# GpSimd's share of the weight splits, and the order in which the last DeltaNet head puts out its results

## The chip, the core and the metric

The kernel runs as one program on one core of a Trainium2 chip. The metric is the device time of one execution in microseconds; the median of several runs counts. A profile of one execution shows what each engine does: TensorE (PE, with its weight loads as PEld), VectorE (DVE), ScalarE (ACT), GpSimd (POOL) and SyncE (SP), which issues the transfers.

## The reference

Two blocks work one after the other on 256 tokens `x` and 256 tokens of context, each 1024 wide. The first block has two layers of latent attention, a Fourier mix, a Hyena convolution and a squared-ReLU feed-forward net (FFN). The second block has two layers as well. Its first one is a DeltaNet with an FFN, for `x` and for its context; its second one is a gated linear attention (GLA) with an FFN, of which only `x` is put out. The change lies around the DeltaNet, of which this is the core, for chunks of tokens in order:

```python
sol = triangular_solve(eye + m, rhs)          # m: beta * k k^T * decay, strictly lower
v_new = u - einsum('bhid,bhdv->bhiv', w, s)
o = (einsum('bhid,bhdv->bhiv', qc * exp(gcum)[..., None], s)
     + einsum('bhij,bhjv->bhiv', a_qk, v_new))
s = s * exp(gcum[..., -1:])[..., None] + einsum('bhjd,bhjv->bhdv', kc * tail[..., None], v_new)
```

It runs forwards and backwards, first over the context, whose last state `s` starts the run over `x`. Then `o` of both directions is added, normalised over its 128 values, multiplied by `silu(z)` and by the output weights, and added to the stream. After that each stream is normalised over its 1024 values and goes into the FFN, `square(relu(h @ w1)) @ w2`.

## The kernel before

Activations lie with their 1024 features over 128 partitions and 8 slices; the two streams stand side by side in 512 columns, `x` in 0 to 255 and the context in 256 to 511 (`st`, each with its index of the modulation). The dense products are made as three products of rounded parts: `weight` (line 297) loads a block of 128 x 1024 floats into one of three raw buffers, ScalarE rounds it into `wh` (line 307), and line 308 forms the rest, `wl = raw - wh`. That second step is here called a split. It is made by GpSimd if the caller says `pool` or the stage says `pool_lo`, else by VectorE. `mm3` multiplies `wh` with both parts of the input and `wl` with the first, so a block of eight slices and 512 columns takes 24 matmuls.

The order of the instructions on each engine is made by a scheduler when the kernel is built. It takes what is ready by its own estimate of time, in the order of the program where several are ready; each engine then runs its list strictly in that order, and waits where an operand isn't there. `issue_after` sets single instructions behind another one of their engine.

GpSimd makes 91 of the splits: 63 in the DeltaNet (`pool_lo=True` in `run`) and 28 outside, namely the first four blocks of each of the four FFNs (16), the first blocks of the stage that follows an FFN (2 for the first block's second layer, 2 for the DeltaNet, 2 for the GLA), and six of the GLA's projections. It also makes some products of the DeltaNet's `prepare` (lines 1254 and 1256), some of the GLA, and parts of the norm (line 516).

The DeltaNet has eight pairs of heads, called heads here. `project` makes keys, queries and two value tiles of a head (four blocks, each convolved over five taps by VectorE, line 1171), `gates` its two gate tiles (two blocks), `prepare` the decays and the inverse of the small triangular parts (a chain on VectorE, then two trips through memory, `dout` into `TT`, line 1291), `merge` doubles the inverse in three levels, and `steps` runs the four chunks in both directions. `scale` squares the results on ScalarE, takes the inverse root by a chain of small VectorE instructions (`rsqrt`, lines 432 to 438) and multiplies (line 1416). `readout` transposes them, multiplies by the gate and splits them into two parts (tag `r`, four buffers). `write_out` multiplies with two blocks of the output weights and adds to the stream by VectorE (`finish`, line 659). The loop runs over `hd`: merge and steps of head `hd`, `prepare` of the next, `write_out` of the one before, `project` of the one after the next, `readout`, and `gates` of the next.

At `hd == 6` only the first gate tile of the last head is made. The second one and the `write_out` of head six are cut into 24 parts of three matmuls of 512 columns (`late`), which stand between the instructions of head seven's merge (6 parts) and steps (10 parts, line 1388); what is left (8 parts) follows behind `scale`. Then `readout` of head seven needs the four `r` buffers that the parts have read. `write_out(7, og, S, then)` goes over `x` first and the context second: for each, eight results of six matmuls of 256 columns, `finish` with squares and sums for the norm, and then the norm itself (`then`, by `norm_one`). The FFN's first four blocks are multiplied by `lins`, `x` first.

Of the kernel before, what the change touches and what calls it, by code (L numbers as in the profile page):

```python
# [18 lines left out]
P = 128  # L19
# [185 lines left out]
class Net:  # L205
# [91 lines left out]
    def weight(self, src, into=None, pool=False, ahead=False):  # L297
        shp = list(src.shape)
        raw = self.wp.tile(shp, F32, tag="wr", bufs=self.nr_, name="wr")
        self.nc.sync.dma_start(raw, src)  # L300
        wp, nw = (self.wp2, 4) if self.wp2 and not ahead else (self.wp, self.nw)
        if into:
            hi, lo = into
        else:
            hi = wp.tile(shp, F32R, tag="wh", bufs=nw, name="wh")
            lo = wp.tile(shp, F32R, tag="wl", bufs=nw, name="wl")
        self.nc.scalar.copy(hi, raw)  # L307
        (self.nc.gpsimd if pool or self.pool_lo else self.nc.vector).tensor_tensor(lo, raw, hi.bitcast(F32), ALU.subtract)  # L308
        return hi, lo
# [10 lines left out]
    def lin(self, src, rhs, n0, n1, w=None, pool=False):  # L320
        w = w or self.weight(src, pool=pool)
# [231 lines left out]
    def ffn(self, xs, g, w1, w2, mod, tag, streams, ys=None, h=None, quota=0, every=1, S=None, scales=None, before=None, then=None):  # L553
        one = len(streams) == 1
        with ExitStack() as st:
# [5 lines left out]
            ws = [self.weight(self.a[w1][m], pool=True) for m in range(4)]  # L561
# [8 lines left out]
            self.mlp(xs, h, ws, w1, w2, mod, 5, streams, S, scales or {"xc"[v]: 1.0 for (_, _, v) in streams}, before, then, nS)  # L570
# [4 lines left out]
    def mlp(self, xs, h, ws, w1, w2, mod, gch, streams, S, scales, before, then, nS):  # L575
        nc = self.nc
        n = 256 * len(streams)
        for s in range(4):
# [3 lines left out]
            for m in range(0, 8, 2):  # L582
# [13 lines left out]
                elif s == 0 and m == 0:  # L596
                    first = self.lins(ws[:4], h, streams)
# [73 lines left out]
    def pools(self, st, sb, ps, nr, pm, quota=0, pool_lo=False, nwm=2, wide=4, low=()):  # L671
        self.n += 1
        self.pool_lo = pool_lo
# [394 lines left out]
    def deltanet(self, xs, mod, h, ws, first):  # L1068
# [249 lines left out]
        def merge(hd, c, parts):  # L1318
# [30 lines left out]
        def steps(hd, c, parts):  # L1349
# [4 lines left out]
            for step in range(4):  # L1354
                Sn = ap.tile([P, 512], F32, tag="S", bufs=2, name="S") if step < 3 else None
                for d in range(2):
# [31 lines left out]
                    self.between(parts, i.ins, 2 if step == 3 else 1)  # L1388
# [13 lines left out]
                S = Sn  # L1402
            return ot

        def scale(c, ot):
            ss = sp.tile([P, 4, 2], F32, tag="ss", name="ss")
            jk = junk()
            for ch in range(4):
                for v in range(2):
                    nc.scalar.activation(jk, ot[ch // 2][:, 256 * (ch % 2) + P * v : 256 * (ch % 2) + P * v + P], AF.Square,  # L1410
                                         accum_out=ss[:, ch, v : v + 1])
            nc.vector.scalar_tensor_tensor(ss, ss, 1.0 / 128, c["aq"].unsqueeze(2).to_broadcast([P, 4, 2]), ALU.mult, ALU.add)
            so = self.rsqrt(ss.rearrange("p c v -> p (c v)"), [P, 8], "o")
            for p in range(2):
                o = ot[p].rearrange("p (c i) -> p c i", i=P)
                nc.vector.tensor_tensor(o, o, so[:, 4 * p : 4 * p + 4].unsqueeze(2).to_broadcast([P, 4, P]), ALU.mult)
# [11 lines left out]
        def write_out(hd, og, S=None, then=None):  # L1428
            ws = [self.weight(a["dwout"][hd, mq]) for mq in range(2)]
            for sv in st if S else [(0, 512, 0)]:  # L1430
                for m in range(8):
                    c = slice(P * (m % 4), P * (m % 4) + P)
                    wh, wl = ws[m // 4]
                    ps = self.mm_ps()[:, : sv[1] - sv[0]]
                    self.mm3(ps, (wh[:, :, c], wl[:, :, c]), og, sv[0], sv[1])
                    if S:
                        self.finish(xs, m, ps, mod, 2, sv, S, dict(x=1.0, c=1.0))
                    else:
                        for s2 in st:
                            self.finish(xs, m, ps[:, s2[0] : s2[1]], mod, 2, s2, None, None)  # L1440
                if then:
                    then(sv)
# [5 lines left out]
        og, parts = None, iter(())  # L1448
        for hd in range(8):
            if hd == 7:  # L1450
                parts = late(zs, og)
            merge(hd, c, parts)
            ot = steps(hd, c, parts)
            if hd < 7:
                nxt = prepare(hd + 1, *proj)
            if 0 < hd < 7:
                write_out(hd - 1, og)
            if hd < 7:
                tokens(nxt)
# [11 lines left out]
            if hd < 6:  # L1471
                zs = gates(hd + 1)
            elif hd == 6:
                zs = zn
            if hd < 7:
                c = nxt
# [4 lines left out]
        write_out(7, og, S, f["then"])  # L1481
# [4 lines left out]
    def gla(self, xs, mod, h, ws):  # L1486
# [46 lines left out]
        w3 = self.weight(win[2], [vtile().rearrange("p b n -> p (b n)").rearrange("p (k m) -> p k m", k=8).bitcast(F32R) for _ in range(2)], pool=True)  # L1533
# [388 lines left out]
```

## Time and profile before

| | us |
|---|---|
| median of three runs | 2655.13 |
| lowest and highest of them | 2652.54 and 2656.1 |
| the profiled execution's own time | 2648.67 |
| its span, first to last instruction | 2646.9 |

The profile is of one execution of its own, with 1.8 us outside the span. TensorE is busy 2503.5 us of the span, VectorE 1648.9, ScalarE 1133.1 and GpSimd 370.3. The mean granted clock of TensorE is 0.977. The DeltaNet lies from about 1085 to 1853 us, the FFN behind it begins at 1852, and the GLA begins at about 2235. A busy time is an average over stages; what bounds the kernel is read in each stage from the waits of TensorE.

### The profile page before, as it was taken

The page shows a single profiled execution, that of the slowest core. Times are in us where ns is not written, and L with a number is a line of the kernel's source. Part 1 is how long each engine was busy: PE and PEld are TensorE (multiplying, and loading weights), DVE is VectorE, ACT ScalarE, POOL GpSimd, SP SyncE. Part 2 cuts the span into 40 slices and gives each one's busy share as a digit, 9 for nine tenths or more (in the row PEclk, how much of TensorE's full clock was granted, in tenths as well). Part 3 has the DMA queues.
Part 4 walks back from the last instruction along what each step waited for, and adds up shares of the span by engine and source line. Part 5 has one row for each costly group of instructions (what it writes and reads, how often), then busy time and mean ns, then how long its engine had stood idle before and what let it go on. Part 6 is the DMA issues. An engine that isn't in the chain of part 4 may idle for free. (4 is left out here: it accounts for less than half of the span.)

```text
span 2646.9 us, 40579 instructions
## 1 busy us (share of the span) xinstructions
PE 2503.5 (95%) x15740; PEld 2108.8 (80%) x15740; DVE 1648.9 (62%) x3449; ACT 1133.1 (43%) x2161; POOL 370.3 (14%) x268
## 2 busy tenths in 40 slices
PE   7999999999999999988999999977999999899999
PEld 4866877778886999867778877866877888698899
DVE  5555443333567777887877887767533435677676
ACT  3344333232355545663545444534422324564453
POOL 0000200000100100332333323312000001420100
PEclk8999999999999999999999999988999999999999
DMA  7334566663241466222122211211554522222554
GB/s 266 120 117 147 176 254 236 242 236 117 77 141 52 160 194 197 80 66 53 34 61 65 71 39 52 65 35 56 204 179 160 182 88 71 79 93 73 172 184 154
DMA packets 147105, 334.09 MB, mean 126 GB/s; under 512 B 57134, under 2 KB 68512, under 8 KB 146912
## 3 DMA queue, kind: packets, MB, share of 16 engines
q1 hardware_dynamic: 146656, 331.43, 38.6%
q8 instruction: 124, 2.03, 0.3%
q14 instruction: 69, 0.57, 0.1%
q0 software_dynamic: 256, 0.07, 0.0%
HBM read 327.78 MB, written 3.67 MB: 125 GB/s over the span
## 5 line engine op out<-in xcount | busy, mean ns | idle before, releaser
L307 ACT CAST wh<-wr 128x1024 fp32r<-128x1024 f32 (+1 forms) x421 | 426.1, 1016 | 700.2 <-PE pmm L317 511.4
L318 PE MATMUL pmm<-h,wl 128*128 128x512 f32 (+2 forms) x1800 | 624.6, 347 | 16.3 <-DVE wl L308 8.8
L316 PE MATMUL pmm<-h,wh 128*128 128x512 f32 (+2 forms) x1800 | 628.8, 349 | 6.9 <-ACT E L829 1.9
L317 PE MATMUL pmm<-h,wh 128*128 128x512 f32 (+2 forms) x1800 | 621.3, 345 | 0.0
L308 DVE TENSOR_TENSOR wl<-wr,wh 128x1024 fp32r<-128x1024 f32 (+1 forms) x333 | 392.3, 1180 | 288.8 <-ACT wh L307 282.3
L318 PE MATMUL pmm<-r,wl 128*128 128x256 f32 (+1 forms) x1312 | 444.3, 339 | 5.6 <-DVE wl L308 5.5
L316 PE MATMUL pmm<-r,wh 128*128 128x256 f32 (+1 forms) x1312 | 444.9, 340 | 4.5 <-DVE q L989 1.6
L317 PE MATMUL pmm<-r,wh 128*128 128x256 f32 (+1 forms) x1312 | 444.2, 339 | 0.1
L308 POOL TENSOR_TENSOR wl<-wr,wh 128x1024 fp32r<-128x1024 f32 x88 | 216.5, 2465 | 1383.1 <-ACT wh L307 724.4
L318 PEld LDWEIGHTS pmm<-h,wl 128*128 128x128 f32 x1800 | 346.6, 193 | 59.7 <-DVE wl L308 10.2
L316 PEld LDWEIGHTS pmm<-h,wh 128*128 128x128 f32 x1800 | 346.3, 192 | 53.0 <-issue 7.2
L317 PEld LDWEIGHTS pmm<-h,wh 128*128 128x128 f32 x1800 | 346.7, 193 | 37.1 <-issue 0.8
L316 PEld LDWEIGHTS pmm<-r,wh 128*128 128x128 f32 x1312 | 248.4, 190 | 38.7 <-issue 8.9
L318 PEld LDWEIGHTS pmm<-r,wl 128*128 128x128 f32 x1312 | 248.8, 190 | 32.0 <-DVE wl L308 7.0
L317 PEld LDWEIGHTS pmm<-r,wh 128*128 128x128 f32 x1312 | 249.1, 190 | 23.2 <-issue 1.7
L659 DVE SCALAR_TENSOR_TENSOR xs<-pmm,modb,xs 128x256 f32<-128x256 f32 x232 | 106.6, 477 | 133.0 <-PE pmm L318 133.0
L659 DVE SCALAR_TENSOR_TENSOR xs<-pmm,moda,xs 128x256 f32<-128x256 f32 x120 | 54.4, 480 | 146.7 <-PE pmm L318 146.5
L294 ACT CAST r<-h 128x256 fp32r<-128x256 f32 (+1 forms) x128 | 65.5, 513 | 126.8 <-DVE h L610 67.2
L295 DVE TENSOR_TENSOR r<-h,r 128x256 fp32r<-128x256 f32 (+1 forms) x128 | 72.9, 570 | 44.1 <-ACT r L294 40.7
L394 PE MATMUL pmd<-wm,cvs 128*32 128x256 f32 x1408 | 87.2, 382 | 0.0
L1371 ACT COPY e<-pa 128x256 f32<-128x256 f32 x64 | 23.8, 371 | 128.5 <-PE pa L1369 128.0
L394 PEld LDWEIGHTS pmd<-wm,cvs 128*32 128x32 f32 x1408 | 41.1, 109 | 40.1 <-issue 13.4
(484 smaller groups left out, 3834.7 us busy)
## 6 DMA issues: line engine op xcount, KB each, us to landing
wr<-w SPq DMA_DIRECT2D x128, 512.0 KB
wr<-f SPq DMA_DIRECT2D x128, 512.0 KB
wm<-amod SPq DMA_DIRECT2D x24, 2048.0 KB
wr<-dwin SPq DMA_DIRECT2D x49, 512.0 KB
wm<-wmod SPq DMA_DIRECT2D x12, 2048.0 KB
wr<-win SPq DMA_DIRECT2D x28, 512.0 KB
wm<-wmod SPq DMA_DIRECT2D x8, 1536.0 KB
wr<-gwin SPq DMA_DIRECT2D x17, 512.0 KB
```

The lines of the kernel that those rows point to most:

```text
L294: self.nc.scalar.copy(hi, src)
L295: self.nc.vector.tensor_tensor(lo, src, hi.bitcast(F32), ALU.subtract)
L307: self.nc.scalar.copy(hi, raw)
L308: (self.nc.gpsimd if pool or self.pool_lo else self.nc.vector).tensor_tensor(lo, raw, hi.bitcast(F32), ALU.subtract)
L316: mm(ps, wh[:, k, :], rh[:, n0:n1], start=k == 0, stop=False)
L317: mm(ps, wh[:, k, :], rl[:, n0:n1], start=False, stop=False)
L318: self.mark = mm(ps, wl[:, k, :], rh[:, n0:n1], start=False, stop=k == last)
L394: self.last = nc.tensor.matmul(ps[32 * c : 32 * c + 32, :256], cs[:, k + i, :], raw[:, i, 256 * c : 256 * c + 256], start=k + i == 0, stop ...
L659: self.nc.vector.scalar_tensor_tensor(x, ps, mod[:, 8 * gch + m, v : v + 1], x, ALU.mult, ALU.add)
L1371: nc.scalar.copy(vA, ptr[:, :256])
```

## The change

GpSimd's splits outside the DeltaNet go to VectorE (all `pool=True` are taken out). In the DeltaNet `pool_lo` is set by the loop, `0 < hd < 6`: the splits of the turns one to five stay with GpSimd, five turns with eight blocks each, 40 in all. Those ahead of the loop, of turn zero, of turn six and of all that follows go to VectorE. So 51 splits move.

The last head leaves the loop. Both its gate tiles are made in turn six, and `late` keeps only the `write_out` of head six: 16 parts, six of them in the merge and four in steps zero and one. As soon as step one has ended, when both directions have passed the context's chunks, `scale` runs for the context alone, and the one for `x` behind step three. New functions read out one stream (`readout1`, into four free buffers with the tag `D` in place of `r`) and write out one stream (`write_last`). The order is then: context read out, the parts that are left, the context's output product, `x` read out, the context's norm, the output product of `x`, its norm. The FFN's `lins` takes the context first.

The core of the diff; the lines left out take away further `pool` arguments, here and in `run`, and pass `order` on:

```diff
-    def weight(self, src, into=None, pool=False, ahead=False):
+    def weight(self, src, into=None, ahead=False):
...
-        (self.nc.gpsimd if pool or self.pool_lo else self.nc.vector).tensor_tensor(lo, raw, hi.bitcast(F32), ALU.subtract)
+        (self.nc.gpsimd if self.pool_lo else self.nc.vector).tensor_tensor(lo, raw, hi.bitcast(F32), ALU.subtract)
...
-                f["ws"] = [self.weight(w, pool=True, ahead=True) for w in win]
+                f["ws"] = [self.weight(w, ahead=True) for w in win]
...
-            ws = [self.weight(self.a[w1][m], pool=True) for m in range(4)]
+            ws = [self.weight(self.a[w1][m]) for m in range(4)]
...
-                    first = self.lins(ws[:4], h, streams)
+                    first = self.lins(ws[:4], h, order)
...
-        def late(zs, og):
-            def use(ps):
-                zs.append(ap.tile([P, 512], F32, tag="vf", bufs=2, name="z"))
-                nc.scalar.activation(zs[1], ps, AF.Silu)
-
-            yield from self.lin_parts(lambda: self.weight(win[48]), h, 512, use)
+        def late(og):
...
-                    self.between(parts, i.ins, 2 if step == 3 else 1)
+                    if step < 2:
+                        self.between(parts, i.ins)
...
                 S = Sn
+                if step == 1 and half:
+                    half(ot)
             return ot
...
+        def scale(c, ot, streams=(0, 1)):
+            n = len(streams)
...
+            c0 = 2 * streams[0]
+            for ch in range(2 * n):
...
+        def readout1(ot, zs, og, p):
+            pt = self.b_ps()
+            sl = slice(256 * p, 256 * p + 256)
+            for v in range(2):
+                for j in range(2):
+                    self.transpose(pt[:, C(2 * v + j)], ot[p][:, 256 * j + P * v : 256 * j + P * v + P])
+            for v in range(2):
+                z = zs[v][:, sl]
+                nc.vector.scalar_tensor_tensor(z, pt[:, 256 * v : 256 * v + 256], dng[:, 0:1], z, ALU.mult, ALU.mult)
+                self.split(og[v][0][:, sl], og[v][1][:, sl], z)
...
+        def write_last(ws, og, sv, S):
+            for m in range(8):
+                c = slice(P * (m % 4), P * (m % 4) + P)
+                ps = self.mm_ps()[:, :256]
+                self.mm3(ps, [w[:, :, c] for w in ws[m // 4]], og, sv[0], sv[1])
+                self.finish(xs, m, ps, mod, 2, sv, S, dict(x=1.0, c=1.0))
...
-        for hd in range(8):
...
+        for hd in range(7):
+            self.pool_lo = 0 < hd < 6
+            merge(hd, c)
+            ot = steps(hd, c)
...
-            elif hd == 6:
-                zn = [gate(7, 0)]
             else:
-                for part in parts:
-                    part()
+                zn = gates(7)
...
+        parts = late(og)
+        merge(7, c, parts)
+        ot = steps(7, c, parts, lambda ot: scale(c, ot, (1,)))
+        scale(c, ot, (0,))
+        D = lambda: ap.tile([P, 4, P], F32, tag="D", bufs=8, name="og").rearrange("p s i -> p (s i)").bitcast(F32R)
+        og = [(D(), D()) for _ in range(2)]
...
-        write_out(7, og, S, f["then"])
+        readout1(ot, zs, og, 1)
+        for part in parts:
+            part()
+        ws = [self.weight(a["dwout"][7, mq]) for mq in range(2)]
+        write_last(ws, og, st[1], S)
+        with self.tc.issue_after(self.mark.ins):
+            readout1(ot, zs, og, 0)
+        f["then"](st[1])
+        write_last(ws, og, st[0], S)
+        f["then"](st[0])
```

## Rows read from the trace of the kernel before

**Rows 1.** The page: busy us, share of the span, instructions.

```profile
PE 2503.5 (95%) x15740; PEld 2108.8 (80%) x15740; DVE 1648.9 (62%) x3449; ACT 1133.1 (43%) x2161; POOL 370.3 (14%) x268
```

**Rows 2.** Busy time of the engines in four stretches.

```profile
core 0: us, PE busy (x) PEld busy (x) DVE busy (x) ACT busy (x) POOL busy (x), PEclk, DMA share, GB/s
1085.00:1258.00 173.00, 150.11 (x799) 122.68 (x797) 138.43 (x281) 91.27 (x191) 61.11 (x35) 0.93 0.22 61
...
1747.00:1790.00 43.00, 29.38 (x178) 24.84 (x178) 20.52 (x39) 9.96 (x17) 2.34 (x1) 0.80 0.14 25
1813.00:1853.00 40.00, 24.66 (x147) 22.18 (x145) 33.34 (x80) 18.30 (x46) 14.76 (x7) 0.78 0.25 79
...
1880.00:1900.00 20.00, 20.00 (x89) 16.52 (x88) 14.17 (x18) 10.99 (x16) 0.00 (x0) 1.00 0.77 266
```

**Rows 3.** Waits of TensorE, 1813 to 1853 us.

```profile
PE pb L452 <- DVE ot L1416: 11.2, 1, 11.2
PE pb L458 <- DVE rsy L438: 1.6, 1, 1.6
PE pmm L316 <- ACT r L294: 1.1, 1, 1.1
PE pmm L350 <- ACT h L515: 1.0, 1, 1.0
```

**Rows 4.** Timeline, 1818 to 1830 us, VectorE and GpSimd.

```profile
1819.95 0.15 DVE L437 TENSOR_TENSOR rst<-rst,rsh 128x8 f32<-128x8 f32 x1
...
1820.18 9.25 POOL L308 TENSOR_TENSOR wl<-wr,wh 128x1024 fp32r<-128x1024 f32 x4 [2.30 <-ACT wh L307]
...
1824.88 2.27 DVE L437 TENSOR_TENSOR rst<-rst,rsh 128x8 f32<-128x8 f32 x1
```

**Rows 5.** The chain that ended last, 1812 to 1853 us: start, us, what.

```profile
1813.10 0.26 ACT junk L1410
...
1815.66 0.41 ACT junk L1410 x2
...
1833.27 1.01 PE pmm L316 x3
...
1838.63 0.21 PE pmm L318
...
1842.15 0.12 PE pmm L316
...
1852.97 0.58 PE pmm L351
```

**Rows 6.** Waits of TensorE, 1740 to 1790 us.

```profile
PE pb L452 <- DVE ot L1416: 5.9, 1, 5.9
PE pa L1333 <- DMA TT<-dout: 3.6, 1, 3.6
```

**Rows 7.** Line 308: count, then ns as min/median/max.

```profile
L308 DVE TENSOR_TENSOR wl<-wr,wh x333: 409/1225/3355, 50.7 to 2635.3; 128x1024 fp32r<-128x1024 f32 x155, 128x384 fp32r<-128x384 f32 x8, 128x256 fp32r<-128x256 f32 x4
...
L308 POOL TENSOR_TENSOR wl<-wr,wh x88: 2338/2404/3402, 286.8 to 2461.8; 128x1024 fp32r<-128x1024 f32 x88
```

**Rows 8.** Timeline, 1153 to 1157 us, VectorE and GpSimd.

```profile
1153.41 2.40 POOL L308 TENSOR_TENSOR wl<-wr,wh 128x1024 fp32r<-128x1024 f32 x1 [4.96 <-DMA din<-Mt]
...
1153.95 3.10 DVE L1171 SCALAR_TENSOR_TENSOR kq<-pmm,dcw,kq 128x508 f32<-128x508 f32 x4 [2.65 <-ACT kq L1166]
```

**Rows 9.** Waits of TensorE, 1085 to 1258 us.

```profile
PE pmm L318 <- POOL wl L308: 4.7, 1, 4.7
...
PE pb L452 <- DVE vt L1312: 2.8, 1, 2.8
```

**Rows 10.** Waits of TensorE, 870 to 900 us.

```profile
PE pmm L318 <- DVE wl L308: 2.1, 1, 2.1
```

**Rows 11.** Waits of TensorE, 2245 to 2316 us.

```profile
PE pmm L318 <- POOL wl L308: 2.6, 1, 2.6
```

**Rows 12.** Waits of TensorE, 2440 to 2466 us.

```profile
PE pmm L318 <- DVE wl L308: 4.4, 1, 4.4
```

More of the change, by code (lines that the diff above doesn't have):

```diff
@@ L318, in mm3, with lin @@
             self.mark = mm(ps, wl[:, k, :], rh[:, n0:n1], start=False, stop=k == last)
-    def lin(self, src, rhs, n0, n1, w=None, pool=False):
-        w = w or self.weight(src, pool=pool)
+    def lin(self, src, rhs, n0, n1, w=None):
+        w = w or self.weight(src)
         ps = self.mm_ps()
@@ L549, in residual, with ffn @@
                                                 xs[:, m, c0:c1], ALU.mult, ALU.add)
-    def ffn(self, xs, g, w1, w2, mod, tag, streams, ys=None, h=None, quota=0, every=1, S=None, scales=None, before=None, then=None):
+    def ffn(self, xs, g, w1, w2, mod, tag, streams, ys=None, h=None, quota=0, every=1, S=None, scales=None, before=None, then=None, order=None):
         one = len(streams) == 1
@@ L569, in ffn, with mlp @@
                 h = self.norm_mod(xs, streams, self.gscale(mod, 4, g, tag), mod, 3, ys, "n", self.hr(), True)
-            self.mlp(xs, h, ws, w1, w2, mod, 5, streams, S, scales or {"xc"[v]: 1.0 for (_, _, v) in streams}, before, then, nS)
+            self.mlp(xs, h, ws, w1, w2, mod, 5, streams, S, scales or {"xc"[v]: 1.0 for (_, _, v) in streams}, before, then, nS, order or streams)
             self.background(999)
             self.wp2 = None
-    def mlp(self, xs, h, ws, w1, w2, mod, gch, streams, S, scales, before, then, nS):
+    def mlp(self, xs, h, ws, w1, w2, mod, gch, streams, S, scales, before, then, nS, order):
         nc = self.nc
@@ L667, in finish, with pools @@
                 S["next"](m)
[L671 removed]
+    def pools(self, st, sb, ps, nr, pm, quota=0, nwm=2, wide=4, low=()):
         self.n += 1
[L673 removed]
+        self.pool_lo = False
         self.wp2 = None
@@ L1315, in tokens, with merge @@
             c["vt"] = vt
-        def merge(hd, c, parts):
+        def merge(hd, c, parts=iter(())):
             Mt, TT = c["Mt"], c["TT"]
@@ L1346, in merge, with steps @@
                     nc.vector.tensor_tensor(mix(TT[1], 4 * hf, 4, s), v4(FT), v4(pzt), ALU.subtract)
-        def steps(hd, c, parts):
+        def steps(hd, c, parts=iter(()), half=None):
             kq, vt, D, mbt, ktm, TB = c["kq"], c["vt"], c["D"], c["mbt"], c["ktm"], c["TT"][1]
@@ L1447, in deltanet @@
         proj = project(1)
-        og, parts = None, iter(())
-        for hd in range(8):
[L1450 to L1456, printed above, removed]
+        og = None
+        for hd in range(7):
+            self.pool_lo = 0 < hd < 6
+            merge(hd, c)
+            ot = steps(hd, c)
+            nxt = prepare(hd + 1, *proj)
+            if hd:
                 write_out(hd - 1, og)
-            if hd < 7:
-                tokens(nxt)
+            tokens(nxt)
             scale(c, ot)
@@ L1530, in gates @@
                 yield cums, tots
-        w3 = self.weight(win[2], [vtile().rearrange("p b n -> p (b n)").rearrange("p (k m) -> p k m", k=8).bitcast(F32R) for _ in range(2)], pool=True)
+        w3 = self.weight(win[2], [vtile().rearrange("p b n -> p (b n)").rearrange("p (k m) -> p k m", k=8).bitcast(F32R) for _ in range(2)])
         ps, ps1 = self.lins(ws, h, st)
@@ L1556, in values @@
         def values(hd):
-            w = [self.weight(a["gwv"][hd, kh], pool=False) for kh in range(2)]
+            w = [self.weight(a["gwv"][hd, kh]) for kh in range(2)]
             vs = vtile()
@@ L1780, in early @@
                             self.background(2)
-                            ws = [self.weight(a["win_0"][m], pool=False) for m in (8, 9)]
+                            ws = [self.weight(a["win_0"][m]) for m in (8, 9)]
                             self.background(5)
@@ L1821, in before @@
                             f["gs"] = gs
-                            f["ws"] = [self.weight(a["dwin"][m], pool=True, ahead=True) for m in range(2)]
+                            f["ws"] = [self.weight(a["dwin"][m], ahead=True) for m in range(2)]
                         if s == 3.5:
@@ L1873, in before @@
                 self.follow(f, xs, S, gs, mods2[1][0], 0, "n", [a["gwin"][m] for m in range(2)])
-        self.ffn(xs, "fg_0", "f1_0", "f2_0", mods2[0][0], "4", both, None, h, 12, 4, S, None, before, lambda sv: f["then"](sv))
+        self.ffn(xs, "fg_0", "f1_0", "f2_0", mods2[0][0], "4", both, None, h, 12, 4, S, None, before, lambda sv: f["then"](sv), [both[1], both[0]])
         self.dump("slay0", xs)
```

51 lines of the change are left out of this document (19 added, 32 removed).

## The prediction

> **What bounds the kernel now.** I read the page first: TensorE is busy in 95% of the span, VectorE in 62%, GpSimd in 14% [rows 1]. That leaves some 143 us in which TensorE stands still, and the question is how much of it lies where the change works. The stretches tell that. Where the FFN behind the DeltaNet runs, TensorE fills 20 of 20 us at the full clock [rows 2], so nothing is to be had there. In the DeltaNet's first two heads (1085 to 1258 us) it is busy 150 of 173 us at a mean granted clock of 0.93, between 1747 and 1790 us 29.4 of 43 at 0.80, and between 1813 and 1853 us 24.7 of 40 at 0.78 [rows 2]. The reader is to see two things in these rows: the idle time of TensorE, and that its clock falls in the same stretches, so that what it then does takes longer as well. A result of six matmuls of 256 columns advances by 0.21 us a matmul right after the long pause, and by 0.12 a few us later [rows 5]: the levels of 1.2 and 2.4 GHz.
>
> The waits say what the idle time waits for. At the end of the last head TensorE waits 11.2 us for `ot` of line 1416, then 1.1, 1.6 and 1.0 us for the links of readout and norm: 14.9 us [rows 3]. The timeline shows what stands behind the 11.2: four of the small instructions of the inverse root, which took 0.15 us a moment before, take up to 2.27 us each, exactly while GpSimd makes four splits in a row for the FFN, 9.25 us in all [rows 4]. So the chain isn't long by its work; VectorE stands still beside GpSimd. Before the merge of the last head there are waits of 5.9 us, for the same line beside another split, and of 3.6 us for the transfer of `TT` [rows 6].
>
> **What VectorE pays for GpSimd's splits.** A split takes 2.40 us on GpSimd and 1.23 on VectorE [rows 7], so the 51 moved ones bring VectorE 51 x 1.23 = 63 us of work. What it gets back are stalls. They do not strike every instruction: four convolution taps, with one operand in PSUM and one in SBUF, take 3.10 us beside a split, 0.78 each [rows 8], while the small instructions with two operands in SBUF stand until the split ends [rows 4].
>
> The Trainium skill, page "SBUF — State Buffer", section "Who interferes with whom", states this as a rule: a VectorE instruction with two inputs in SBUF contends with a GpSimd instruction that reads SBUF, the later one waits until the first has ended, and one with at most one such input does not contend. Rows 4 and 8 agree. By the rule alone each moved split could give back up to 2.40 us of stall, 51 x (2.40 - 1.23) = 60 us of VectorE's time, an estimate; the rows show stalls on the way of TensorE only in the places above and below, and the sum goes by those.
>
> **The change, part by part.** *The end of the last head.* Today's chain runs from the first square at 1813.1 us to the first output matmul at 1833.3: 20.2 us [rows 5]. Without the stalls it loses some 8.3 us, at most 4 x (2.27 - 0.15) = 8.5, as the splits for the FFN leave GpSimd [rows 4]. For `x` alone four pairs of squares instead of eight save 4 x 0.41 = 1.6 us [rows 5], and half of the multiplication, of the transposes and of the parting save about 1.8, an estimate from the 3.8 us between the end of the stalls (1829.5) and the first matmul. So `x` needs some 8.5 us behind the last step. What covers it: six parts of three matmuls at 0.225 us (89 in 20 us [rows 2]), 4.1 us, and the context's output product, 48 matmuls at 0.12, 5.8 us [rows 5]. 9.9 us of cover are more than 8.5, so the 11.2 us and the 1.1 us go, if the context's own readout is through by then; its scale runs beside steps two and three. The clock then has no pause to fall in: of the output products' 96 matmuls some 27 ran at 0.21 instead of 0.12, and 27 x 0.09 = 2.4 us go too. Then the norm: today the chain leaves the output products at 1842.2 us, and 10 us later TensorE is about to run the FFN (1852 [rows 5]); in their place the context's norm has `x`'s product beside it, 5.8 us. The rest, 4.2 us, is an upper bound for the idle time there, against 2.6 now [rows 3]; I take 3, a loss of 0.4. The context goes into the FFN first, and `x` has the 96 matmuls of the context's four blocks, some 11 us, for its norm. Sum of this part: 11.2 + 1.1 + 2.4 - 0.4 = 14.3 us less.
>
> *The second gate tile.* Its 24 matmuls, 5.4 us, move from the gaps of the last head into turn six, where 9.5 us stand idle [rows 6]. That fills 5.4 of them. What it vacates was partly wait-filling: of the eight parts fewer, two stood behind the steps (1.4 us, on the path), six between the steps, where the chain of the recurrence may take as long without them. Bounds 1.4 and 5.4; I take 3, as TensorE was busy 29.4 of 43 us there and hence the chain, not TensorE, sets the pace for a good part. The clock of 0.80 between 1747 and 1790 us [rows 2] should rise with the pause halved; half of the 0.2 x 43 = 8.6 us is a bound, 2 us my value, since a chain that waits for others gains little from a faster TensorE.
>
> *What VectorE takes on there.* Two splits of the last output weights and four of the FFN, 6 x 1.23 = 7.4 us, in a stretch where it is busy 33.3 of 40 us, 8.3 of that stalled [rows 2, 4]. They may stand ahead of the chain in its queue, and behind them `ot`, the sums and the norm. Bounds 0 and 7.4; I take 2. The end of the DeltaNet therefore gives 14.3 + 3 + 2 - 2 = 17.3 us.
>
> *The first two heads.* 15 blocks' splits move: two of the first projection's early blocks, one more of it, two gate blocks, and four, four and two of the next turns. VectorE is busy 138 of 173 us there [rows 2]; 15 x 1.23 = 18.5 us come in. Against it stand TensorE's waits for a split on GpSimd, 4.7 us, and for `vt`, 2.8 us, which stood behind a multiplication that shared its time with a split [rows 9]. With 35 us free in VectorE's stretch and some stalls gone, I take 6 us less. Bounds: the idle time in which the splits had a hand, with the clock, 15 us less; all 18.5 us on the path and nothing back, 18.5 more. Nearest to the row of 4.7, a gain.
>
> *The rest.* Of the 23 moved splits in the DeltaNet the eight of turn six and behind it are two of output weights counted above and six that lie in or behind turn six, where TensorE has projections to do while they are made: 0 on the path, and inside the 2 us above if late. Of the 28 outside, four are the FFN's above; four before the first FFN and six that are loaded ahead of a stage lie where TensorE has work: 0. Three places are left. Before the second FFN TensorE waits 2.1 us for a split on VectorE [rows 10], in the GLA 2.6 us for one on GpSimd [rows 11], before the last FFN 4.4 us for one on VectorE, which took 3.36 us instead of 1.23 beside GpSimd's [rows 7, 12]. I take 2 us each, bounds 4 less and 3 more each. Turns one to five keep their splits: 0.
>
> Sum: 17.3 + 6 + 3 x 2 = 29.3, say 29 us less. From the profiled execution's own 2648.67 us that gives 2619.7; the median of the runs stands 6.5 us above it, so I predict 2655.13 - 29 = 2626 us.
>
> **The rivals.** *VectorE bounds the end as well (2639 us).* The scheduler puts the FFN's splits, the sums and the context's norm between the links of `x`'s chain, or the context's readout comes too late to cover anything. Then the new order gives nothing, and only the removed stall of 8.3 us and the filled pause remain: 8.3 + 3 - 2 = 9.3, with 6 + 1 elsewhere (VectorE being the tight one there too, the three places give 1 in place of 6) some 16 us less. For it speaks that VectorE has 25 us of true work in these 40 us and gets 7.4 more; against it that part of the context's share is done beside the steps.
>
> *The first two heads pay (2649 us).* VectorE is 80% busy there; if two thirds of the 18.5 us end on the path and the stalls give nothing, the start loses 12, the end gains 17, the rest 1: 6 us less.
>
> *VectorE becomes the bound wherever it takes a split (2665 us, slower).* The place is its queue, in order: behind a split that waits for its rounding on ScalarE stand the sums, the taps and the inverse's chain, and TensorE waits for these. All 63 us on the path, 17 + 8 given back by the end and by its stalls, 28 by the stalls of the other places: 10 us more. It decides from about 43 of the 51 splits on the path, 53 us, the sum of what comes back. Against it: between 1813 and 1853 us a stall, not the work, filled VectorE [rows 4].
> The Trainium skill, page "Perfetto Trace Analysis", section "Optimizing Scalar/DVE Operations", speaks for this rival: with VectorE saturated, moving work to GpSimd may make sense, which the change undoes; the same passage doubts it for the shared port. No row here shows VectorE without slack over a whole head.
>
> **How the numbers follow.** Chances: forecast 0.62 (own range 2614 to 2640), VectorE at the end 0.18, the first heads 0.11, slower 0.09. Faster means by over 0.2%, 5.3 us, about what a measurement of this kernel can tell: the first two and half of the third, 0.85; same 0.06; slower 0.09. The range reaches from the best of all bounds, 17 + 6 for the end with the clock, 15 in the first heads and 9 of the 12 elsewhere, 47 less (2608), to where the first heads pay: 2648.
>
> **What would show it.** Right: no VectorE instruction of 128 x 8 above 0.3 us at the last head's end; no wait above 4 us there; from the last step to the FFN's first matmul some 20 us instead of 40; GpSimd's splits 40, VectorE's 51 more; the clock near 1 from 1747 us on. Wrong: new waits of TensorE for `wl` of line 308 on VectorE in the first heads, a longer stretch up to head two, or a wait for `ot` or for the first `h` of the context that grows into what the stall has left.

## The result, and the profile after

The changed kernel takes 2616.64 us, median of four runs (2615.32 to 2620.0), the kernel before 2653.84 beside it: 37.2 us less, a ratio of 0.9861 with a 95% interval of 0.9844 to 0.9878. The forecast was 2626, 29 us less. The profiled execution took 2615.32 us with a span of 2613.6, which is 33.3 us less than the one before; the stretches below add up to that.

The page first, which answers to [rows 1]:

```profile
PE 2493.7 (95%) x15740; PEld 2100.6 (80%) x15740; DVE 1650.7 (63%) x3517; ACT 1136.8 (43%) x2165; POOL 235.9 (9%) x217
```

GpSimd lost 134 us, VectorE took 51 splits and is busy 1.8 us longer. The new order adds 17 small instructions to VectorE, so the cleaner row is that of the first experiment below (e1), which has just the 51 splits more:

```profile
PE 2490.9 (95%) x15740; PEld 2102.3 (80%) x15740; DVE 1649.5 (63%) x3500; ACT 1136.8 (44%) x2163; POOL 238.0 (9%) x217
```

The splits alone are 63 us of work and VectorE is busy 0.6 us longer, so some 62 us of stall came back, 1.2 us for each split moved, half of the 2.40 us that the prediction allowed at most.

The same stretches as in [rows 2], and a steady turn (1446.5 to 1533.3 us); columns as there:

```profile
1086.00:1243.00 157.00, 143.51 (x796) 117.77 (x794) 134.27 (x294) 93.29 (x192) 25.91 (x21) 0.97 0.25 67
1446.50:1533.30 86.80, 83.11 (x487) 69.08 (x486) 68.91 (x164) 41.75 (x106) 28.30 (x16) 1.00 0.22 57
1728.00:1771.00 43.00, 36.87 (x223) 30.61 (x222) 26.32 (x55) 14.35 (x34) 0.00 (x0) 0.96 0.20 48
1793.00:1822.00 29.00, 16.38 (x108) 15.48 (x106) 27.69 (x81) 17.52 (x43) 2.91 (x4) 0.79 0.28 91
```

The first two heads shrank from 173 to 157 us. TensorE's idle time there fell from 22.9 to 13.5 us, and its own work from 150.1 to 143.5, as the granted clock rose from 0.93 to 0.97. Before the last head's steps the clock rose from 0.80 to 0.96. At the end it didn't (0.78 and 0.79), and VectorE is busy 27.7 of 29 us there.

The waits of TensorE at that end, 1790 to 1823 us, which answer to [rows 3]:

```profile
PE pmm L350 <- DVE xs L659: 7.1, 1, 7.1
PE pb L452 <- DVE ot L1417: 4.3, 1, 4.3
PE pmm L316 <- DVE xs L659: 0.7, 2, 0.5
PE pmm L316 <- ACT og L294: 0.5, 1, 0.5
```

The wait for `ot` fell from 11.2 to 4.3 us but didn't go, and a new one of 7.1 us stands before the FFN's first matmul. Together 12.6 us, where there were 14.9. The timeline of VectorE shows what the new one is for:

```profile
1818.02 0.41 DVE L503 TENSOR_TENSOR e<-xs,pb 128x256 f32<-128x256 f32 x1
1818.35 0.47 DVE L501 SCALAR_TENSOR_TENSOR e<-xs,gs,pb 128x256 f32<-128x256 f32 x1
1818.74 0.55 DVE L512 SCALAR_TENSOR_TENSOR h<-e,modb,h 128x256 fp32r<-128x256 f32 x1
1819.22 0.41 DVE L477 TENSOR_TENSOR acc<-acc,sq 128x256 f32<-128x256 f32 x1
1819.55 0.47 DVE L659 SCALAR_TENSOR_TENSOR xs<-pmm,modb,xs 128x256 f32<-128x256 f32 x1
1819.95 0.90 DVE L512 SCALAR_TENSOR_TENSOR h<-e,modb,h 128x256 fp32r<-128x256 f32 x1
1820.76 0.47 DVE L659 SCALAR_TENSOR_TENSOR xs<-pmm,modb,xs 128x256 f32<-128x256 f32 x1
```

The output product of `x` left TensorE at 1814.3, but its last two additions (line 659) stand in VectorE's queue behind the context's norm (lines 501 to 512). TensorE's FFN waits until the second one has read its PSUM buffer: line 350 starts at 1821.38.

In the first two heads the largest wait is now for a split on VectorE, 4.2 us. The prediction had named such a wait as a sign of being wrong; it stands where 4.7 us for a split on GpSimd stood [rows 9], and the stretch is shorter all the same. In the merge of the last head only the transfer is left, with waits below 1 us. These two groups of waits (1086 to 1243 and 1728 to 1771 us) answer to [rows 9] and [rows 6]:

```profile
PE pmm L318 <- DVE wl L308: 4.2, 1, 4.2
PE pa L1364 <- DVE e L1360: 2.3, 1, 2.3
PE pb L452 <- DVE vt L1307: 1.7, 1, 1.7
...
PE pa L1328 <- DMA TT<-dout: 3.2, 1, 3.2
```

Line 308 over the whole kernel, as in [rows 7]: no split on VectorE takes more than 1.74 us now (3.36 before), and GpSimd keeps 40.

```profile
L308 DVE TENSOR_TENSOR wl<-wr,wh x381: 409/1225/1742, 49.1 to 2602.0; 128x1024 fp32r<-128x1024 f32 x179, 128x384 fp32r<-128x384 f32 x8, 128x256 fp32r<-128x256 f32 x4
...
L308 POOL TENSOR_TENSOR wl<-wr,wh x40: 2356/2406/2482, 1218.6 to 1668.8; 128x1024 fp32r<-128x1024 f32 x40
```

### The profile page after: what moved, and what is told of

Read it like the earlier page. It is cut to its first block, busy times and chain, and to the rows that moved or that the text cites. A ratio compares the mean times of both kernels' runs of the same rounds, so it can differ in the third digit from the quotient of the medians.

```text
span 2613.6 us, 40590 instructions
## 1 busy us (share of the span) xinstructions
PE 2493.7 (95%) x15740; PEld 2100.6 (80%) x15740; DVE 1650.7 (63%) x3517; ACT 1136.8 (43%) x2165; POOL 235.9 (9%) x217
## 5 line engine op out<-in xcount | busy, mean ns | idle before, releaser
L308 DVE TENSOR_TENSOR wl<-wr,wh 128x1024 fp32r<-128x1024 f32 (+1 forms) x381 | 448.8, 1179 | 316.8 <-ACT wh L307 310.0
L316 PE MATMUL pmm<-r,wh 128*128 128x256 f32 (+1 forms) x1280 | 436.3, 342 | 3.0 <-DVE q L989 1.6
L318 PE MATMUL pmm<-r,wl 128*128 128x256 f32 (+1 forms) x1280 | 434.9, 340 | 2.2 <-DVE wl L308 2.1
L317 PE MATMUL pmm<-r,wh 128*128 128x256 f32 (+1 forms) x1280 | 433.9, 339 | 0.0
L316 PEld LDWEIGHTS pmm<-h,wh 128*128 128x128 f32 x1800 | 342.1, 190 | 56.2 <-issue 7.1
L317 PEld LDWEIGHTS pmm<-h,wh 128*128 128x128 f32 x1800 | 342.6, 190 | 39.6 <-issue 0.8
L316 PEld LDWEIGHTS pmm<-r,wh 128*128 128x128 f32 x1280 | 241.3, 189 | 36.0 <-issue 8.9
L318 PEld LDWEIGHTS pmm<-r,wl 128*128 128x128 f32 x1280 | 241.5, 189 | 28.4 <-DVE wl L308 3.4
L317 PEld LDWEIGHTS pmm<-r,wh 128*128 128x128 f32 x1280 | 241.9, 189 | 22.7 <-issue 1.7
L516 POOL TENSOR_TENSOR h<-n,h 128x256 fp32r<-128x256 f32 x28 | 21.7, 776 | 1153.5 <-ACT h L515 1153.5
L308 POOL TENSOR_TENSOR wl<-wr,wh 128x1024 fp32r<-128x1024 f32 x40 | 96.2, 2405 | 146.8 <-ACT wh L307 112.9
```

What stands on the lines that cost most here:

```text
L308: (self.nc.gpsimd if self.pool_lo else self.nc.vector).tensor_tensor(lo, raw, hi.bitcast(F32), ALU.subtract)
L316: mm(ps, wh[:, k, :], rh[:, n0:n1], start=k == 0, stop=False)
L317: mm(ps, wh[:, k, :], rl[:, n0:n1], start=False, stop=False)
L318: self.mark = mm(ps, wl[:, k, :], rh[:, n0:n1], start=False, stop=k == last)
L516: (nc.gpsimd if pool and j in (0,2,4,6) else nc.vector).tensor_tensor(lo, t, hi.bitcast(F32), ALU.subtract)
```

## The experiments

Each kernel was timed against the kernel before in the same session. The median of the kernel before differed between sessions (2651.18 to 2653.18 us), so kernels of different sessions are compared by their ratios. Where a stretch is given, it runs between marks that each kernel has: a matmul of the same number, and the first matmul with `S` and `kq` in each head's steps. All stretches are of profiled executions. The total ahead of the DeltaNet isn't read: e5 and e7, which are the same in TensorE's list up to the DeltaNet's end but for line numbers, differ there by 4 us.

**e1, the splits alone; e2, the order alone.** e1 is the kernel before with

```diff
-        (self.nc.gpsimd if pool or self.pool_lo else self.nc.vector).tensor_tensor(...)
+        (self.nc.gpsimd if self.pool_lo else self.nc.vector).tensor_tensor(...)
...
+            self.pool_lo = 0 < hd < 6      # first line of the loop over hd; False ahead of it
```

e2 is the changed kernel with the `pool` arguments of before put back and `pool_lo` true from the DeltaNet's first `project` on. Two splits made ahead of that stay with VectorE, so GpSimd makes 89 in e2 and not 91.

> The kernel before with the 51 splits moved as in the change and nothing else: old order, x first, last head in the loop. If the stalls of VectorE beside GpSimd were the cost (theory A), the first two heads give their 17 us here too, the four FFN splits no longer stall the inverse root at the end (8 us), and the GLA and the last FFN give some 5: about 2624 us, and the wait for ot at the end of the last head shrinks from 11.2 us to about 3. If the new order is what pays (theory B), only the small places outside give something: about 2645 us.

> The changed kernel with all 91 splits on GpSimd again, so the new order alone. Theory A (stalls): the first two heads are as long as before (173 us between the marks), the wait for ot at the end stays above 8 us, and only the pause before the last merge is filled (about 9 us): some 2644 us. Theory B (order): about 2625 us.

e1 took 2616.31 us, ratio 0.9861 (0.9847 to 0.9874): all of the gain. e2 took 2655.62, ratio 1.0012 (1.0001 to 1.0023): none; theory A had foreseen 2644 for it. By stretches, us against the kernel before:

| stretch | forecast | the change | e1, splits | e2, order |
|---|---|---|---|---|
| up to the DeltaNet | -2 | +2.1 | +1.6 | +6.4 |
| its start, to the first step of head one | -6 | -17.1 | -17.5 | +5.7 |
| to the first step of head six | 0 | +4.0 | +0.3 | +3.7 |
| to the last step of head seven | -5 | -9.1 | -7.8 | -3.6 |
| into the FFN | -12.3 | -9.3 | -4.0 | -3.3 |
| GLA, to the last FFN | -4 | -4.1 | -6.5 | -2.7 |
| sum, with the rest | -29.3 | -33.3 | -33.8 | +6.2 |

So theory A holds, and e1 even came out 8 us below the 2624 that it foresaw, although the wait for `ot` at the end is 6.3 us, 4.9 less than before but not 3. At the end the two parts support each other: -4.0 and -3.3 apart, -9.3 together. What the order alone won there it lost elsewhere: 5.7 us at the start, where with all but two of the splits as before the wait for `vt` grew from 2.8 us [rows 9] to 7.1, and 3.7 us in the turns one to five, whose code it doesn't touch. e5 and e6 take these up.

**e3 and e10, the DeltaNet's start.** The changed kernel with

```diff
+        self.pool_lo = True                # ahead of project(0)
-            self.pool_lo = 0 < hd < 6
+            self.pool_lo = hd < 6          # e3; e10 keeps 0 < hd < 6
```

> The changed kernel with the splits of the DeltaNet's preamble and of turn zero on GpSimd again (15 of them). Theory A: the start loses its whole gain of 17 us, in waits for vt, FT, row and for a split on GpSimd: about 2634 us, everything behind it as in the changed kernel. Rival: the gain of the start comes from the order in which the scheduler now happens to set the instructions, not from where these splits are: within 4 us of 2617.

> The changed kernel with only the splits made ahead of the loop on GpSimd again (the first head's projection and gates and the second head's projection), those of turn zero on VectorE. In e3 both groups together cost 20 us. If the loss is by stalls, and the stalls lie where VectorE prepares the first head alone, with nothing else for TensorE to do, most of it shows here: about 2630 us. Rival: it lies in turn zero, whose splits stand beside the merge and steps of the first head: about 2620 us.

e3 took 2637.19 us, ratio 0.9941 (0.9928 to 0.9953), 0.8 points above the change, some 21 us: the whole gain of the start is lost, and a little more. GpSimd makes 53 splits in it, so 13 went back and not 15; the first two stay with VectorE as in e2. Of the waits, those for `vt`, `FT`, `row` and a split on GpSimd were foreseen, those for `g` and `Y` were not. TensorE's waits in e3, 1086 to 1258 us:

```profile
PE pb L452 <- DVE vt L1307: 5.6, 1, 5.6
PE pb L1240 <- ACT g L1234: 5.5, 1, 5.5
PE pmm L318 <- POOL wl L308: 3.3, 1, 3.3
PE pa L1340 <- ACT FT L1325: 2.1, 1, 2.1
PE pa L1335 <- DVE Y L1331: 2.0, 1, 2.0
PE pb L1240 <- DVE row L1152: 2.0, 1, 2.0
```

e10 took 2637.54, ratio 0.9944 (0.993 to 0.9957): the seven splits ahead of the loop cost it all, and in sum those of turn zero add nothing to them. Its window, 172 us long, has the old clock again and VectorE as busy as in the changed kernel's 157 us:

```profile
1086.00:1258.00 172.00, 151.49 (x827) 125.68 (x826) 134.28 (x302) 92.08 (x200) 45.26 (x28) 0.93 0.22 61
```

**e4, the four FFN splits; e11, the eight of turn six and behind it.** The changed kernel with

```diff
-            ws = [self.weight(self.a[w1][m]) for m in range(4)]
+            ws = [self.weight(self.a[w1][m], pool=tag == "4") for m in range(4)]     # e4
-            self.pool_lo = 0 < hd < 6
+            self.pool_lo = 0 < hd                                                    # e11
```

> The changed kernel with only the four splits for the FFN behind the DeltaNet on GpSimd again. Stall theory: the small instructions of the inverse root and the sums with two operands in SBUF stand still beside the 9.2 us of splits; the wait for ot of x grows from 4.3 to about 10 us: some 2624 us. Rival: at the end VectorE is bound by its queue, and 4 x 1.22 = 4.9 us less in it bring the FFN's first matmul forward by 3 to 5 us: about 2613 us.

> The changed kernel with the splits of turn six and of all behind it in the DeltaNet on GpSimd again (eight). Stretch from head six's steps to head seven's: 64 us in the changed kernel, 72.6 before, 64.9 with the splits alone (e1), 69.7 with the order alone (e2). Stall theory: this stretch grows back by 5 to 6 us, and the output weights' splits stall the last head's end by 2 to 4: about 2624 us. Rival (the second gate tile and not the splits shortened it): within 2 us of 2617.

e4 took 2619.94 us, ratio 0.9878 (0.9862 to 0.9893). By the ratios that is 4.5 us more than the change, but the intervals overlap. The trace says it more plainly, though the cost is smaller than foreseen (2624 us and a wait of 10): the stretch from the last step into the FFN is 6.4 us longer, and the wait for `ot` 7.7 in place of 4.3 us (the first line; the norm's wait, second, is nearly what it was):

```profile
PE pb L452 <- DVE ot L1417: 7.7, 1, 7.7
PE pmm L350 <- DVE xs L659: 6.5, 1, 6.5
```

So here too the stalls cost more than VectorE saves by giving the work away. e11 took 2625.94, ratio 0.9902 (0.9888 to 0.9915), some 11 us above the change. From head six's first step to head seven's it needs 72.0 us (64.1 in the change, 72.6 before), and from the last step into the FFN 3.0 us more. In a window of its own around the first of these stretches (60 us in the change, 68 in e11), TensorE's idle time grows by 3.4 us and its busy time by 4.6, as the granted clock falls from 0.97 to 0.92.

**e5, the old addresses; e6, the splits at the new ones; e7, the norm behind.** The steady turns took 86.1 us before and in e1, 86.8 in the kernels with the new order (e5, e7 and e9 apart, of which below). Their idle time is the same, but TensorE's starts of 512-column matmuls from `h` lie 232 ns apart instead of 227 (medians). The new order draws small tiles from new tags (`ss1`, `ss2`, and those of the inverse root), which push `h` and all that is placed behind it 128 bytes on. e5 draws them from the old tags:

```diff
-            ss = sp.tile([P, 2 * n, 2], F32, tag=f"ss{n}", name="ss")
+            ss = sp.tile([P, 4, 2], F32, tag="ss", name="ss")[:, : 2 * n]
...
-            so = self.rsqrt(ss.rearrange("p c v -> p (c v)"), [P, 4 * n], f"o{n}")
+            so = self.rsqrt(ss.rearrange("p c v -> p (c v)"), [P, 4 * n], "o")   # in rsqrt: a [P, 8] tile, cut to size
```

e6 is e1 with a tile of 128 bytes ahead of `h`. e7 is e5 with

```diff
-        f["then"](st[1])
+        y = self.stat_end(S, "xc"[st[1][2]])
         write_last(ws, og, st[0], S)
+        f["then"](st[1], y)
         f["then"](st[0])
```

> The changed kernel with the small tiles of scale and of the inverse root drawn from the old tags and cut to size, so that no new small tile stands ahead of the big tile h; h and all behind it lie at the byte addresses of the kernel before again (in the changed kernel they lie 128 bytes further on). Address theory: the products of 512 columns from h in the DeltaNet go back from 232 to 227 ns, a steady turn from 86.85 to 86.1 us, the whole kernel to some 2611 us. Rival (the 232 ns come from the order of the instructions around them): turn and spacing stay, 2617 us.

> The kernel before with the 51 splits moved (e1) and a tile of 128 bytes put ahead of h, which is filled once and never used, so that h and all behind it lie 128 bytes further on. Address theory: 232 ns a matmul and 86.85 us a steady turn, some 2621 us against 2616 of e1. Rival: nothing changes, 2616 us.

> e5 with one thing more: the inverse root of the context's norm is still made ahead of the output product of x, but its multiplications, which are VectorE's, stand behind that product in the program. Theory: the wait of 7.1 us before the FFN's first matmul is for the last two additions of x, which stand in VectorE's queue behind the context's norm; with these ahead the wait falls to 2 or 3 us, and the time to 4 us below e5, some 2607 us. Rival: VectorE has no slack there at all, so that the FFN only waits for its input in place of its buffer: within 1.5 us of e5.

e5 took 2608.56 us, ratio 0.9842 (0.9829 to 0.9856); e6 2622.11, ratio 0.9892 (0.9879 to 0.9906), against 0.9861 (0.9847 to 0.9874) of e1. The same steady turn of the kernel before (first) and of e5, columns as in [rows 2]:

```profile
1459.80:1545.90 86.10, 82.40 (x487) 69.03 (x486) 68.90 (x164) 41.71 (x106) 28.65 (x16) 1.00 0.21 58
1444.50:1530.60 86.10, 82.39 (x487) 69.05 (x486) 68.88 (x164) 41.73 (x106) 28.66 (x16) 1.00 0.21 58
```

The same turn of e6:

```profile
1447.60:1534.50 86.90, 83.19 (x487) 69.20 (x487) 68.88 (x164) 41.80 (x106) 28.27 (x16) 1.00 0.21 58
```

The same 487 matmuls take 82.39 and 83.19 us, with the same work on the other engines. The spacing went back to 227 ns in e5 and up to 232 in e6. The address theory holds both ways round. Of the 8 us between the spans of e6 and e1, 3.7 lie in the turns one to five, and 1.9 ahead of the DeltaNet, where the products of 512 columns in the first 300 us show the same 232 ns in place of 227. The rest lies in the GLA and at the last FFN, where their lists of instructions differ a little.

e7 took 2603.37, ratio 0.9825 (0.9811 to 0.9839), 5.2 us below e5 at its side. The intervals overlap a little, but the trace agrees: from the last step to the FFN's first matmul e5 takes 30.0 us and e7 25.7. The wait of 6.8 us for line 659, which e5 still has, is gone, and 1.7 us for the sums of `x` are left; the other rows are as in the change:

```profile
PE pb L452 <- DVE ot L1417: 4.2, 1, 4.2
PE pb L446 <- DVE acc L477: 1.7, 1, 1.7
```

**e8, the places outside.** The changed kernel with `pool=True` again at the first blocks of the other three FFNs, the blocks loaded ahead and six of the GLA.

> The changed kernel with the 24 splits outside the DeltaNet and the FFN behind it on GpSimd again (the other three FFNs' first blocks, the blocks loaded ahead, six of the GLA). Theory A (waits for GpSimd's slow splits and VectorE's stalls beside them): the GLA and the last FFN lose their 4 to 5 us, the start of the second FFN gains 1 to 2 back: about 2620 us. Rival: these places are hidden and what they gave is chance of the order: 2617 us.

e8 took 2623.84, ratio 0.9896 (0.9881 to 0.9911), some 9 us above the change. From the GLA's beginning to the last FFN's it is 5.0 us longer than the change; most of the rest lies ahead of the DeltaNet, where totals of single executions can't be told apart. TensorE's wait before the last FFN, 2420 to 2440 us, is what it was in [rows 12]:

```profile
PE pmm L318 <- DVE wl L308: 4.3, 1, 4.3
```

In the changed kernel it is 1.0 us. Before the second FFN nothing is won by either: there the change waits 4.3 us for `xs` of line 477 and 1.0 for a split, e8 4.3 for a split and 1.6 for `xs`.

**e9, no split on GpSimd at all.** `self.pool_lo = False` in the changed kernel's loop.

> The changed kernel with the 40 splits of turns one to five on VectorE too, so that GpSimd makes none in the whole kernel. Stall theory carried on: each turn has 8 x 2.4 = 19 us of GpSimd's splits beside VectorE's work; with them gone VectorE saves its stalls and pays 8 x 1.23 = 9.8 us; a turn is set by TensorE (84 of 86.9 us busy), so it stays within 1 us a turn: 2612 to 2620 us. Rival (VectorE becomes the bound wherever it takes a split): VectorE goes from 70 to near 80 of 87 us and TensorE waits for it at the splits, some 2 to 6 us more a turn: 2627 to 2645 us.

e9 took 2604.69, ratio 0.982 (0.9806 to 0.9833), some 11 us below the change. A steady turn of it:

```profile
1443.70:1527.30 83.60, 82.11 (x486) 69.88 (x486) 70.12 (x173) 41.67 (x106) 9.26 (x8) 1.00 0.21 59
```

VectorE makes nine instructions more in the turn, eight splits among them (9.8 us), and is busy 70.1 us where it was 68.9: 8.6 us of stall went. TensorE stands idle 1.5 us a turn in place of 3.7, and the turn is 3.2 us shorter than in the change; that TensorE's own time falls by 1.0 as well, at the same 232 ns, isn't explained. Both theories were wrong in their price: the turn wasn't hidden by TensorE, and VectorE didn't become the bound. Only turn zero lost 6 us, with one wait of 3.9 us for `FT` in it.

**e12, idle work on GpSimd.** The changed kernel with four subtractions behind the squares of `x`, whose results nobody reads:

```diff
+        i = nc.gpsimd.tensor_tensor(MT()[:, :4], ss, ss, ALU.add)
+        with self.tc.issue_after(i.ins):
+            for _ in range(4):
+                nc.gpsimd.tensor_tensor(MT(), k2, k2, ALU.subtract)      # k2: kq of the last head, 128 x 1024
```

> The changed kernel with four subtractions of 128 x 1024 floats added on GpSimd, which start when the squares of x have been summed in the last head; their results are used by nobody, and VectorE keeps all its work. A stall by itself, with no exchange of work. Stall theory: the inverse root's instructions with two operands in SBUF and the sums beside them stand still while GpSimd works (about 9.5 us); TensorE's wait for ot of x grows from 4.3 us by 6 to 10 us, the time to about 2624 us. Rival (a slow VectorE queue is the whole cost, GpSimd does it no harm): the wait stays at 4.3 us.

It took 2613.94 us, ratio 0.9863 (0.9847 to 0.988): no slower than the change. The stall is there all the same. GpSimd's row in its timeline:

```profile
1797.44 7.70 POOL L1494 TENSOR_TENSOR dum<-kq 128x1024 f32<-128x1024 f32 x4 [0.16 <-issue]
```

VectorE's rows beside it:

```profile
1797.46 0.47 DVE L659 SCALAR_TENSOR_TENSOR xs<-pmm,modb,xs 128x256 f32<-128x256 f32 x1
1797.85 1.51 DVE L433 TENSOR_SCALAR rsy<-rsy 128x4 int32<-128x4 int32 x1
1799.28 0.47 DVE L659 SCALAR_TENSOR_TENSOR xs<-pmm,modb,xs 128x256 f32<-128x256 f32 x1
1799.67 1.53 DVE L436 TENSOR_TENSOR rst<-rsy 128x4 f32<-128x4 f32 x1
1801.13 0.41 DVE L477 TENSOR_TENSOR acc<-acc,sq 128x256 f32<-128x256 f32 x1
1801.46 1.84 DVE L437 TENSOR_TENSOR rst<-rst,rsh 128x4 f32<-128x4 f32 x1
```

Four instructions of 0.15 us took 1.5 to 1.8 each (the fourth, line 438, follows at 1803.63 with 1.53): 5.8 us of stall by 7.7 us of work that has nothing to do with them. Each of the four ends within 0.03 us of the end of one of the four subtractions (1799.34, 1801.19, 1803.29 and 1805.14). And the chain pays for it. From line 1413 to the start of line 1417, which makes `ot`, it takes 6.1 us in the change (first two lines), with one of the FFN's splits in between, and 11.3 in e12, without one:

```profile
1796.97 0.16 DVE L1413 SCALAR_TENSOR_TENSOR ss<-ss,aq 128x4 f32<-128x4 f32 x1 [0.57 <-ACT junk L1411]
1803.02 0.68 DVE L1417 TENSOR_TENSOR ot<-ot,rsy 128x512 f32<-128x512 f32 x1
...
1796.85 0.15 DVE L1413 SCALAR_TENSOR_TENSOR ss<-ss,aq 128x4 f32<-128x4 f32 x1
1808.10 0.68 DVE L1417 TENSOR_TENSOR ot<-ot,rsy 128x512 f32<-128x512 f32 x1
```

The kernel's time didn't follow, so neither expectation came true. The additions of line 659, which stand behind the stalled instructions in VectorE's queue, held TensorE up earlier (5.7 us), so that its wait for `ot` was only 1.2. And the scheduler, which knew of the new work, listed the instructions behind it differently: three of the FFN's four splits come after its first matmul, and the wait before that is 1.9 us, for `h`. So the run shows the stall by itself and what it does to the chain, but not its price in the kernel's time.

## Why the prediction was right, and where its steps were off

*Mechanism: right.* VectorE paid for GpSimd's splits in stalls, and the splits moved are worth the whole gain: e1 moves them alone and has it, and e3, e4, e8, e10 and e11 each put some back and lost (e4 by its trace alone). e12 shows the stall with nothing else exchanged. Moving a split also makes the split itself faster, 1.2 us in place of 2.4, and no run parts this from the stalls in the kernel's time. That the stalls weigh more is argued from the waits: in the first two heads the wait for a split only went from 4.7 us on GpSimd to 4.2 on VectorE, and the other waits made the difference.

*The sum: in part luck.* The forecast was 8 us too small by the medians and 4 by the profiled executions. By the table the start and turn six gave 15 us more than forecast, and the end, the turns one to five and the part ahead of the DeltaNet 11 us less; misses of both signs partly cancelled.

*The signs.* GpSimd's splits are 40, VectorE's 51 more, and no small instruction of the inverse root at the end takes more than 0.16 us, as foreseen. Three signs failed: waits of 7.1 and 4.3 us stand at the end, where none above 4 was to be; from the last step to the FFN's first matmul it is 30.3 us, not 20 (41.1 before); and the clock is 0.79 there.

*The first two heads: right in sign, too small.* I took 6 us with a bound of 15; it was 17.1, beyond the bound. Two things were under-sized. The idle time that went was 9.4 us, not 6. The clock, which I had put into the bound only, gave 6.6 more, by TensorE's busy time in the two windows. e10 shows that the splits ahead of the loop carry it all.

*Turn six and the last merge: too small, and the wrong cause.* I took 3 us for the second gate tile and 2 for the clock and costed the splits of turn six at 0, as "TensorE has projections to do". The stretch gained 9.1. e1, without the gate tile's move, gained 7.8 of it, and e11 lost 8 by putting those splits back. The step that failed is the 0. What the gate tile's move gave shows elsewhere: from head six's first step to head seven's the change has 24 matmuls more than e1 in the same time (64.2 and 64.9 us), and fewer are left for the end.

*The end of the last head: 9.3 us in place of 12.3.* That the 8.3 us of stall go was right. But most of what the stretch lost is work and not waiting: up to the FFN's first matmul (the table's mark lies further on) TensorE starts 116 matmuls in place of 151, which take 17.7 us in place of 25.9, and its idle time only falls from 15.2 to 12.6. The step that failed is the cover, on both sides. I counted 9.9 us of it, but the six parts had run by 1792.6, before `x`'s chain began, and the context's product ended at 1799.5, 6.2 us into the chain. And I gave `x`'s chain 8.5 us from the last step, and from the last addition to `ot` (1793.3) to its first output matmul (1806.07) it took 12.8, with additions, sums and a split between its links. This is the first rival's mechanism, in part. So 4.3 us stayed, and with the pause the slow clock: `x`'s first matmuls (1806 to 1809.7) again lie 0.21 us apart. The norm, for which I took a loss of 0.4, lost 4.5, for a reason that I hadn't looked for: a buffer held by an addition in VectorE's queue. e7 shows it by taking it away.

*The rest: 4.1 of 4 us in the GLA and before the last FFN, by luck; before the second FFN no gain.* Of the 4.1 us the GLA gave none (0.4 us longer; the kernels with the same splits there lie between 3.2 less and 0.5 more), and the stretch before the last FFN 5.0 (2.7 to 5.2 in these kernels, none in e2 and e8). Before the second FFN the wait only changed its name.

*Turns one to five, costed at 0: 4.0 us lost.* Not through instructions but through the place of the data.

*The rivals.* "VectorE bounds the end as well" was half true, as above. "VectorE becomes the bound wherever it takes a split" fell, and e9 ends it: VectorE took all 91 and the kernel got faster still. The order by itself gave nothing (e2) and, with the splits moved, 5.3 us at the end against 3.7 lost to addresses; e5, without that loss, lies 5 us below e1 by the ratios, whose intervals overlap.

Fastest were e7 and e9. The two together, with the old addresses, weren't tried. What sets the remaining 4.3 us at the end, splits or sums ahead of the chain, stays open as well.

## What to carry to other kernels

Before giving GpSimd work to relieve VectorE, count what VectorE's instructions take while GpSimd runs, by shape, against the same shapes alone; here a split of 2.4 us on GpSimd cost VectorE about as much as making it. A reordering that frees TensorE must also be followed through the queue of the engine that releases its buffers. And when stretches that an edit doesn't touch get slower with the same waits, look at where their tiles have come to lie.

## What the runs showed of the hardware

The same matmuls of 512 columns start 227 or 232 ns apart, in the DeltaNet's turns, according to whether the tile of their moving data lies at the old address or 128 bytes on; the weights' buffers there had not moved. The first 300 us show the same (227 ns before and in e5, 232 in the change and in e6). In the FFN behind the DeltaNet, where by the order of the pools weights and data had both moved, they stayed at 227 ns. Why is open: a different distance between the two operands, or a place shared with another engine, wasn't tested.

An instruction with a single operand in SBUF stalls too: line 433 took 1.51 us beside GpSimd's subtraction, while additions with one operand in PSUM (line 659, 0.47 us) went on. The Trainium skill, page "SBUF — State Buffer", section "Who interferes with whom", counts this kind of instruction among those that can take both ports and then contend; this run agrees. The prediction told the rule without this exception.

In one place the wait seems to go the other way: in e12 an addition of two operands in SBUF (line 477, 0.41 us at 1801.13) began as one of GpSimd's subtractions ended, and the next of these took 2.14 us in place of 1.90.
